# The input projection's high and low halves in one 512-column product

## The chip, the cores and the metric

The kernel runs on one core of a Trainium2 chip. The metric is the device time of one execution in microseconds. The engines are TensorE (PE in the profile, its weight loads PEld), VectorE (DVE), ScalarE (ACT), GpSimd (POOL) and SyncE (SP), whose queue here issues the transfers.

## The reference

Two layers over 256 tokens of width 2048, batch 1, all in float32:

```python
for l in range(DEPTH):
    h = rms_norm(x, norm_g[l])
    proj = jnp.einsum('btd,dc->btc', h, w_in[l])
    rw_in, g_rw, q, k_at, v_at, g_at = jnp.split(proj, col_splits, axis=-1)
    rw_in = bidir_token_shift(rw_in, shift_mu[l])
    r, k, v, xw, xa = jnp.split(rw_in, rw_splits, axis=-1)
    y_rw = rwkv7_branch(r, k, v, xw, xa, ...)        # two scans, forward and backward, 16 heads
    y_at = window_attention(rope(q), rope(k_at), v_at, sink[l])   # 16 heads, 4 KV heads
    mix = jnp.concatenate([y_rw * jax.nn.silu(g_rw), y_at * jax.nn.silu(g_at)], axis=-1)
    x = x + jnp.einsum('btc,cd->btd', mix, w_out[l])
return rms_norm(x, final_g)
```

The change touches the input projection `proj` (the second line of the loop) and the steps that take its tiles out of PSUM.

## The kernel before

**Precision.** Each float32 operand of a large product is split into a high part (rounded to TensorE's fast float32 type, fp32r) and a low part (the rest). A product is then the sum of three: high weight by high x, high weight by low x, low weight by high x. Every weight tile arrives as float32 and is split on the chip: `wsplit` has ACT write the high part `hi` (L253) and DVE the low part `lo` (L255), in pieces of 128x512.

**The stream.** A tile of the input projection is 128 output columns by 256 tokens, summed over 16 blocks of 128 rows of `w_in`. `gemm` queues a tile as 16 steps, one for each block `kk`, in two halves of 8 with one weight load (512 KB) each. A step of the old form is three products of 256 columns into a `[128, 256]` PSUM tile `pm` (L331, L332, L333). With `wide=True` a step is two products: the high weight by the high and the low part of x in one product of 512 columns (L324), then the low weight by the high part into the first 256 columns (L325); the two halves of the 512-column tile have to be added at the end. The form with `wide` needs both parts of a row side by side. `Pairs` keeps them so, four rows of `(2, 256)` in each of its tiles; `Rows` keeps eight rows of one part in a tile. Before the change only the output projection is `wide`, in its first 15 tiles of 16, with the mixed values `L.M` in `Pairs`; x is in two `Rows`, `L.XH` and `L.XL`, written by `x_split` (ACT L217, DVE L218).

**The tiles of a layer.** Two low-rank tiles (0 and 1); for each of eight pairs of recurrent heads four tiles (k, v, r and gate); the value product of attention (`v_step`, with x as the stationary operand, L600 to L602); two rotary key tiles; eight rotary query tiles and eight gate tiles. When a tile's 16 steps are done, its evacuation runs:

- `shift_evac` (k, v, r and the low-rank tiles): DVE multiplies `pm` by the norm's factor into `u` (L473), ACT scales it into the destination (L474), DVE adds the two shifted neighbours (L475, L476).
- `silu_evac` (gates): DVE multiplies by the norm's factor into `g` (L484), ACT takes a tanh (L485), DVE combines (L486).
- `rope_evac` (rotary): ACT copies `pm` into `u` (L572); four transfers on SP's queue swap its 32-partition blocks into `rrot` (L574); 13 steps later DVE turns it, 15 steps later it is split.

`ps_main` has two buffers for `pm`; the value product takes both at once.

**The order.** TensorE's program is in the order in which the kernel is written. `window(64, ...)` interleaves 64 steps of the stream (four tiles) with stages of the recurrence (`scan_p`, `scan_i`, `scan_b`) and of attention in 11 slots; after 13 such windows a layer's input tiles 2 and on are through. Then come the 256 steps of the output projection and the next layer's tiles 0 and 1. The instructions of DVE and ACT are ordered by the framework's scheduler, from the program order with priority offsets (the low weight parts and `scan_b` are raised). Each engine's queue is served in order.

Of the kernel before, what the change touches and what calls it, by code (L numbers as in the profile page):

```python
# [9 lines left out]
F32 = mybir.dt.float32  # L10
F32R = mybir.dt.float32r
# [4 lines left out]
AF = mybir.ActivationFunctionType  # L16
ALU = mybir.AluOpType
# [116 lines left out]
def hybrid_trunk_kernel(ctx, tc, xT, wi, wv, wo, par, fing, dup, iup, sink, pos, cst, out):  # L134
# [65 lines left out]

    class Pairs:

        def __init__(self):
            self.t = []
            self.more()

        def more(self):
            for tag in (("s0a", "s1a"), ("s0b", "s1b"))[len(self.t) // 2]:
                self.t.append(hold(tag, F32R, "M" + str(len(self.t)), (4, 2, T)))

        def row(self, j, part=None):
            t = self.t[j // 4][:, j % 4]
            return t.rearrange("p a t -> p (a t)") if part is None else t[:, part]

    def x_split(XH, XL, x, k, l):
        g = G0[:, k : k + 1] if l == 0 else PR[:, l, P_NG + k : P_NG + k + 1]
        A.activation(XH[:, k, :], x, AF.Copy, scale=g)  # L217
        V.scalar_tensor_tensor(XL[:, k, :], x, g, XH[:, k, :].bitcast(F32), op0=ALU.mult, op1=ALU.subtract)  # L218

    class Norm:  # L220

# [84 lines left out]

    S = Stream()

    def gemm(src, operands, evac, raws=None, begin=None, bank=None, pairs=None, wide=False):

        box = []

        def step(kk):
            def f(w):
                if not box:
                    box.append(bank() if bank else ps_main.tile([128, 2 * T if wide else T], F32, tag="m", name="pm"))
                    if begin:
                        begin()
                pm = box[0]
                k = kk % 8  # L320
                wh, wl = w[0][:, k * 128 : (k + 1) * 128], w[1][:, k * 128 : (k + 1) * 128]
                if wide:
                    m = pairs()
                    PE.matmul(pm, wh, m.row(kk), start=(kk == 0), stop=(kk == 15), skip_group_check=True)  # L324
                    PE.matmul(pm[:, 0:T], wl, m.row(kk, 0), start=False, stop=(kk == 15), skip_group_check=True)  # L325
                    return
                if pairs:
                    xh, xl = (pairs().row(kk, i) for i in range(2))
                else:
                    xh, xl = (x[:, kk, :] for x in operands())  # L330
                PE.matmul(pm, wh, xh, start=(kk == 0), stop=False)  # L331
                PE.matmul(pm, wh, xl, start=False, stop=False)  # L332
                PE.matmul(pm, wl, xh, start=False, stop=(kk == 15))  # L333
# [127 lines left out]
    def queue_inputs(l):  # L461
# [2 lines left out]
        dpm = lambda o, j: DP[:, l, o + j : o + j + 1]  # L464

        def inproj(ct, evac, **kw):
            gemm(wi[l, ct], lambda: (L.XH, L.XL), evac, **kw)

        def shift_evac(j, place):
            def evac(pm):  # L470
                dst = place()
                u = st("u", [T], bufs=2)
                V.tensor_tensor(u, pm, L.norm.rb, op=ALU.mult)  # L473
                A.activation(dst, u, AF.Identity, scale=dpm(0, j))  # L474
                V.scalar_tensor_tensor(dst[:, 1:T], u[:, 0 : T - 1], prm(P_MU0, j), dst[:, 1:T], op0=ALU.mult, op1=ALU.add)  # L475
                V.scalar_tensor_tensor(dst[:, 0 : T - 1], u[:, 1:T], prm(P_MU1, j), dst[:, 0 : T - 1], op0=ALU.mult, op1=ALU.add)  # L476

            return evac

        def silu_evac(place):  # L480
            def evac(pm):
                g = st("g", [T], bufs=2)
                th = st("g", [T], bufs=2)
                V.tensor_tensor(g, pm, L.norm.rb, op=ALU.mult)  # L484
# [67 lines left out]
            return evac  # L552

        for p, t in enumerate(L.ts):
            inproj(2 + 4 * p, shift_evac(p, new(t, "k", "kr", 4)), begin=ups(p, t))
            inproj(3 + 4 * p, value_evac(p, t))
            inproj(4 + 4 * p, shift_evac(16 + p, new(t, "r", "kr", 4)))
            inproj(5 + 4 * p, silu_evac(new(t, "gr", "vg", 8)))


        rope = []
# [1 line left out]
        def rope_evac(place):  # L563
            def evac(pm):
# [7 lines left out]
                A.activation(raw, pm, AF.Copy)  # L572
                for q in range(4):
                    SY.dma_start(out=rot[q * 32 : q * 32 + 32, :], in_=raw[(q ^ 1) * 32 : (q ^ 1) * 32 + 32, :])  # L574
                hi, lo = place()
# [17 lines left out]
        def v_step(kk, b):  # L593
            def f(w):
                if not pvs:
                    pvs.extend(ps_main.tile([128, T], F32, tag="m", name="pva") for _ in range(2))
                k = kk % 4
                wh, wl = (x[:, k * 256 : (k + 1) * 256] for x in w)
                tb = slice(b * 128, (b + 1) * 128)
                PE.matmul(pvs[b], L.XH[:, kk, tb], wh, start=(kk == 0), stop=False)  # L600
                PE.matmul(pvs[b], L.XH[:, kk, tb], wl, start=False, stop=False)
                PE.matmul(pvs[b], L.XL[:, kk, tb], wh, start=False, stop=(kk == 15))  # L602

            return f

# [19 lines left out]
            return place  # L625

        for m in range(2):
            inproj(2 + 4 * NP + m, rope_evac(k_place(m)))
        L.tq = [dict() for _ in range(8)]

        def q_place(j):
# [8 lines left out]
        for n in ("q0", "q1", "q2", "q3", "g0", "q4", "g1", "q5", "g2", "q6", "g3", "q7", "g4", "g5", "g6", "g7"):  # L640
            j = int(n[1])
            if n[0] == "q":
                inproj(QG0 + 2 * j, rope_evac(q_place(j)))
            else:
                inproj(QG0 + 2 * j + 1, silu_evac(new(L.tq[j], "g", "vg", 8)))

    def queue_output(l):

# [3 lines left out]
        def tile_of(k):  # L652
# [6 lines left out]
            def evac(pm):  # L659
# [7 lines left out]
                if k == 0:  # L667
                    to.norm = Norm()
                    to.acc = st("acc", [T])
                    if not last:  # L670
                        to.XH, to.XL = Rows("s2", F32R, "XH"), Rows("s3", F32R, "XL")
                if not last:
                    x_split(to.XH, to.XL, x, k, l + 1)
# [17 lines left out]

        for k in range(NKT):
            ev, be = tile_of(k)
            gemm(wo[l, k], None, ev, begin=be, pairs=lambda: L.M, wide=k < NKT - 1)

    def layer(l):
        L = layers[l]
        prm = lambda o, j: PR[:, l, o + j : o + j + 1]
        dpm = lambda o, j: DP[:, l, o + j : o + j + 1]
        L.M = Pairs()  # L700
        FR = hold("s0b", F32, "FR", (8 * T,))

        def mix_split(j, y, g2):
# [601 lines left out]
```

## Time and profile before

| | |
|---|---|
| median of 3 runs | 1169.26 us (1168.23 to 1169.78) |
| profiled execution | 1168.46 us, its span 1166.7 us |
| granted TensorE clock | 0.994 |
| TensorE busy, weight loads busy | 1145.5 us (98%), 1051.1 us (90%) |
| DVE busy, ACT busy | 915.9 us (79%), 785.6 us (67%) |
| steps in the old form, reading XH | 1664 |
| steps in the wide form | 480 |

The span is from the first to the last instruction; busy time is the time in which at least one instruction of the engine runs, with the tail in which it overlaps its successor. The duration of a matmul holds its way through the array, which the next one overlaps: what one costs TensorE in a stream is the distance between the starts of two. The windows of layer 0 run from about 23.8 to 496.7 us, those of layer 1 from about 599 to 1066 us; each window takes between 24 and 43 us.

### The profile page before, as it was taken

Reading aid. Unit: us, or ns where it says so; the run is one execution under the profiler, and the core shown is the slowest. Engines: PE = TensorE matmul, PEld = TensorE weight load, DVE = VectorE, ACT = ScalarE, POOL = GpSimd, SP = SyncE. Lnnn points to the kernel's source line nnn. Section 1 sums busy time; section 2 is a strip of 40 time slices with the busy share of each in tenths; the row PEclk is TensorE's granted clock in tenths of the full one; section 3 lists DMA queues with packets and bytes.
Section 4 is the critical chain, followed back from the end, with each engine's and each line's share of the span. In section 5 each row is a group of like instructions: output and inputs, shape, how many; then the busy total and the mean of one; then the engine's idle time right before and its main releaser. Section 6 shows DMA issues by size and latency. Waiting matters only on the chain.

```text
span 1166.7 us, 37155 instructions
## 1 busy us (share of the span) xinstructions
PE 1145.5 (98%) x15671; PEld 1051.1 (90%) x15671; DVE 915.9 (79%) x2042; ACT 785.6 (67%) x1986; POOL 21.7 (2%) x23
## 2 busy tenths in 40 slices
PE   8999999999999999999999999999999999999996
PEld 7998999999899998988899889999999999988885
DVE  7889978888877677767768888888887767786665
ACT  6667876787775666655556677876786666675553
POOL 0000000000000000000000000000000000000000
PEclk9999999999999999999999999999999999999998
DMA  7544434333334443477655443334333344345663
GB/s 261 169 152 134 131 103 130 97 112 111 101 116 123 126 127 122 133 235 242 217 182 171 143 136 116 100 114 126 104 112 112 120 130 130 101 150 184 211 202 126
DMA packets 60551, 166.59 MB, mean 143 GB/s; under 512 B 7744, under 2 KB 22880, under 8 KB 60384
## 3 DMA queue, kind: packets, MB, share of 16 engines
q1 hardware_dynamic: 60384, 164.21, 45.1%
q8 instruction: 123, 2.02, 0.7%
q14 instruction: 44, 0.36, 0.1%
HBM read 157.37 MB, written 4.19 MB: 138 GB/s over the span
## 4 chain that ended last, share of the span: by engine, by line
PE 76%; issue 13%; DVE 5%; ACT 4%; DMA 2%; SPq 0%; POOL 0%; POOLq 0%; DVEq 0%; ACTq 0%
PE pm L331 17%; PE pm L333 14%; PE pm L332 14%; PE pm L324 4%; PE pg L855 3%; PE pm L325 2%; PE pcc L1018 2%; DVE lo L255 2%; PE pcc L1046 2%; PE pd L962 1%; PE py L1030 1%; PE py L1003 1%; PE pq L953 1%; PE pcc L1036 1%; ACT hi L253 1%
## 5 line engine op out<-in xcount | busy, mean ns | idle before, releaser
L255 DVE TENSOR_TENSOR lo<-raw,hi 128x512 fp32r<-128x512 f32 x560 | 371.9, 686 | 103.7 <-ACT hi L253 101.6
L253 ACT ACTIVATE hi<-raw 128x512 fp32r<-128x512 f32 x560 | 329.5, 625 | 167.8 <-PE pm L324 58.4
L331 PE MATMUL pm<-XHa,hi 128*128 128x256 f32 x832 | 245.5, 295 | 0.9 <-ACT VA L609 0.4
L331 PE MATMUL pm<-XHb,hi 128*128 128x256 f32 x832 | 243.6, 293 | 0.2 <-ACT hi L253 0.2
L333 PE MATMUL pm<-XHb,lo 128*128 128x256 f32 x832 | 234.0, 281 | 1.4 <-DVE lo L255 1.4
L333 PE MATMUL pm<-XHa,lo 128*128 128x256 f32 x832 | 234.2, 281 | 1.1 <-DVE lo L255 0.8
L332 PE MATMUL pm<-XLa,hi 128*128 128x256 f32 x832 | 234.2, 282 | 0.5 <-DVE XLa L218 0.3
L332 PE MATMUL pm<-XLb,hi 128*128 128x256 f32 x832 | 234.0, 281 | 0.1
L331 PEld LDWEIGHTS pm<-XHa,hi 128*128 128x128 f32 x832 | 157.0, 189 | 11.6 <-ACT XHa L217 1.7
L324 PE MATMUL pm<-M,hi 128*128 128x512 f32 x480 | 166.9, 392 | 0.4 <-ACT hi L253 0.4
L331 PEld LDWEIGHTS pm<-XHb,hi 128*128 128x128 f32 x832 | 157.2, 189 | 5.9 <-ACT hi L253 0.4
L333 PEld LDWEIGHTS pm<-XHa,lo 128*128 128x128 f32 x832 | 157.2, 189 | 2.4 <-DVE lo L255 2.3
L333 PEld LDWEIGHTS pm<-XHb,lo 128*128 128x128 f32 x832 | 157.2, 189 | 2.1 <-DVE lo L255 2.0
L332 PEld LDWEIGHTS pm<-XLa,hi 128*128 128x128 f32 x832 | 157.3, 189 | 1.1 <-DVE XLa L218 1.1
L332 PEld LDWEIGHTS pm<-XLb,hi 128*128 128x128 f32 x832 | 157.3, 189 | 0.3 <-DVE XLb L218 0.3
L325 PE MATMUL pm<-M,lo 128*128 128x256 f32 x480 | 134.3, 280 | 0.2 <-DVE lo L255 0.2
L324 PEld LDWEIGHTS pm<-M,hi 128*128 128x128 f32 x480 | 90.1, 188 | 21.2 <-issue 0.8
L325 PEld LDWEIGHTS pm<-M,lo 128*128 128x128 f32 x480 | 90.1, 188 | 0.5 <-DVE lo L255 0.5
L1041 ACT ACTIVATE suv<-pcc 64x128 f32<-64x128 f32 x128 | 34.5, 270 | 72.3 <-PE pcc L1039 48.5
L1124 ACT ACTIVATE mv<-mv,mx 128x257 f32<-128x257 f32 x56 | 28.0, 502 | 15.1 <-DVE mx L1121 15.0
L956 ACT ACTIVATE QF<-pq 128x256 f16<-128x256 f32 x80 | 30.4, 380 | 10.5 <-PE pq L920 6.2
L855 PE MATMUL pg<-mv,FR 64*128 64x128 f32 x512 | 37.2, 285 | 0.0
(292 smaller groups left out, 2044.3 us busy)
## 6 DMA issues: line engine op xcount, KB each, us to landing
raw<-wi SPq DMA_DIRECT2D x207, 512.0 KB
raw<-wo SPq DMA_DIRECT2D x64, 512.0 KB
raw<-wv SPq DMA_DIRECT2D x8, 512.0 KB
rrot<-u SPq DMA_DIRECT2D x80, 32.0 KB
vg<-xT SPq DMA_DIRECT2D x16, 128.0 KB
xd<-vg SPq DMA_DIRECT2D x16, 128.0 KB
vg<-xd SPq DMA_DIRECT2D x16, 128.0 KB
g<-dup SPq DMA_DIRECT2D x16, 97.0 KB
```

The lines of the kernel that those rows point to most:

```text
L253: A.activation(hi[:, q], raw[:, q], AF.Copy)
L255: V.tensor_tensor(lo[:, q], raw[:, q], hi[:, q].bitcast(F32), op=ALU.subtract)
L324: PE.matmul(pm, wh, m.row(kk), start=(kk == 0), stop=(kk == 15), skip_group_check=True)
L325: PE.matmul(pm[:, 0:T], wl, m.row(kk, 0), start=False, stop=(kk == 15), skip_group_check=True)
L331: PE.matmul(pm, wh, xh, start=(kk == 0), stop=False)
L332: PE.matmul(pm, wh, xl, start=False, stop=False)
L333: PE.matmul(pm, wl, xh, start=False, stop=(kk == 15))
L855: PE.matmul(pg[:, h, c * 128 : (c + 1) * 128], BK[half[h], d, c, 1 - h : 3 - h, :].rearrange("p s j -> p (s j)"), MV[half[h], d, c].rearra ...
L956: A.activation(t_sub(QF), flat4(pq[:, :, 0:128]), AF.Copy)
L1018: PE.matmul(pc[half[h], 0, d, :], GE[h][r, d, ci[d], 0, :], SUV[r, d, ci[d], h, :], start=True, stop=True)
L1041: A.activation(here(h), pc[half[h], 1], AF.Copy)
L1124: A.activation(Sc[:, h, q, 0:257], Sc[:, h, q, 0:257], AF.Exp, scale=0.125, bias=mx[:, q : q + 1], accum_out=den[:, q : q + 1])
```

## The change

Both parts of x's rows are kept in `Pairs` (`L.X`, in the same memory as before), and `gemm` takes all its rows from a `Pairs`. All tiles but 0 and 1 of each layer run with `wide=True`: the four tiles of each pair and attention's key, query and gate tiles, 50 of 52. At the end of a wide tile ACT copies the second half of `pm` to SBUF and DVE adds the first half to it; in the pairs' and gate tiles that comes ahead of the multiply by the norm's factor, which then reads SBUF (`scaled`), and in the rotary tiles ACT's copy takes the second half and the add follows it. The value product takes its stationary operand from the same rows.

```diff
-        def __init__(self):
-            self.t = []
+        def __init__(self, name, tags):
+            self.name, self.tags, self.t = name, tags, []
             self.more()
 
         def more(self):
-            for tag in (("s0a", "s1a"), ("s0b", "s1b"))[len(self.t) // 2]:
-                self.t.append(hold(tag, F32R, "M" + str(len(self.t)), (4, 2, T)))
+            for s in self.tags:
+                i = len(self.t)
+                self.t.append(hold(s + "ab"[i // 2], F32R, self.name + str(i), (4, 2, T)))
...
-    def x_split(XH, XL, x, k, l):
+    def x_rows():
+        x = Pairs("X", ("s2", "s3"))
+        x.more()
+        return x
+
+    def x_split(X, x, k, l):
         g = G0[:, k : k + 1] if l == 0 else PR[:, l, P_NG + k : P_NG + k + 1]
-        A.activation(XH[:, k, :], x, AF.Copy, scale=g)
-        V.scalar_tensor_tensor(XL[:, k, :], x, g, XH[:, k, :].bitcast(F32), op0=ALU.mult, op1=ALU.subtract)
+        A.activation(X.row(k, 0), x, AF.Copy, scale=g)
+        V.scalar_tensor_tensor(X.row(k, 1), x, g, X.row(k, 0).bitcast(F32), op0=ALU.mult, op1=ALU.subtract)
...
                 if wide:
-                    m = pairs()
+                    m = rows()
                     PE.matmul(pm, wh, m.row(kk), start=(kk == 0), stop=(kk == 15), skip_group_check=True)
                     PE.matmul(pm[:, 0:T], wl, m.row(kk, 0), start=False, stop=(kk == 15), skip_group_check=True)
                     return
...
-            gemm(wi[l, ct], lambda: (L.XH, L.XL), evac, **kw)
+            gemm(wi[l, ct], lambda: L.X, evac, **kw)
+
+        def scaled(o, pm):
+            x = pm
+            if pm.shape[-1] > T:
+                A.activation(o, pm[:, T : 2 * T], AF.Copy)
+                V.tensor_tensor(o, o, pm[:, 0:T], op=ALU.add)
+                x = o
+            V.tensor_tensor(o, x, L.norm.rb, op=ALU.mult)
...
-                V.tensor_tensor(u, pm, L.norm.rb, op=ALU.mult)
+                scaled(u, pm)
...
-                V.tensor_tensor(g, pm, L.norm.rb, op=ALU.mult)
+                scaled(g, pm)
...
-            inproj(2 + 4 * p, shift_evac(p, new(t, "k", "kr", 4)), begin=ups(p, t))
-            inproj(3 + 4 * p, value_evac(p, t))
+            inproj(2 + 4 * p, shift_evac(p, new(t, "k", "kr", 4)), begin=ups(p, t), wide=True)
+            inproj(3 + 4 * p, value_evac(p, t), wide=True)
...
-                A.activation(raw, pm, AF.Copy)
+                A.activation(raw, pm[:, T : 2 * T], AF.Copy)
+                V.tensor_tensor(raw, raw, pm[:, 0:T], op=ALU.add)
...
-                PE.matmul(pvs[b], L.XH[:, kk, tb], wh, start=(kk == 0), stop=False)
+                PE.matmul(pvs[b], L.X.row(kk, 0)[:, tb], wh, start=(kk == 0), stop=False)
...
-            inproj(2 + 4 * NP + m, rope_evac(k_place(m)))
+            inproj(2 + 4 * NP + m, rope_evac(k_place(m)), wide=True)
...
-                inproj(QG0 + 2 * j, rope_evac(q_place(j)))
+                inproj(QG0 + 2 * j, rope_evac(q_place(j)), wide=True)
             else:
-                inproj(QG0 + 2 * j + 1, silu_evac(new(L.tq[j], "g", "vg", 8)))
+                inproj(QG0 + 2 * j + 1, silu_evac(new(L.tq[j], "g", "vg", 8)), wide=True)
```

The pairs' other two tiles (r and gate) get `wide=True` in the same way, and the callers of `x_split` pass the one object.

More of the change, by code (lines that the diff above doesn't have):

```diff
@@ L307, in hybrid_trunk_kernel, with gemm @@
     S = Stream()
-    def gemm(src, operands, evac, raws=None, begin=None, bank=None, pairs=None, wide=False):
+    def gemm(src, rows, evac, raws=None, begin=None, bank=None, wide=False):
         box = []
@@ L326, in f @@
                     return
[L327 to L330, printed above, removed]
+                xh, xl = (rows().row(kk, i) for i in range(2))
                 PE.matmul(pm, wh, xh, start=(kk == 0), stop=False)
@@ L554, in queue_inputs @@
         for p, t in enumerate(L.ts):
-            inproj(2 + 4 * p, shift_evac(p, new(t, "k", "kr", 4)), begin=ups(p, t))
-            inproj(3 + 4 * p, value_evac(p, t))
-            inproj(4 + 4 * p, shift_evac(16 + p, new(t, "r", "kr", 4)))
-            inproj(5 + 4 * p, silu_evac(new(t, "gr", "vg", 8)))
+            inproj(2 + 4 * p, shift_evac(p, new(t, "k", "kr", 4)), begin=ups(p, t), wide=True)
+            inproj(3 + 4 * p, value_evac(p, t), wide=True)
+            inproj(4 + 4 * p, shift_evac(16 + p, new(t, "r", "kr", 4)), wide=True)
+            inproj(5 + 4 * p, silu_evac(new(t, "gr", "vg", 8)), wide=True)
         rope = []
@@ L599, in f @@
                 tb = slice(b * 128, (b + 1) * 128)
-                PE.matmul(pvs[b], L.XH[:, kk, tb], wh, start=(kk == 0), stop=False)
-                PE.matmul(pvs[b], L.XH[:, kk, tb], wl, start=False, stop=False)
-                PE.matmul(pvs[b], L.XL[:, kk, tb], wh, start=False, stop=(kk == 15))
+                PE.matmul(pvs[b], L.X.row(kk, 0)[:, tb], wh, start=(kk == 0), stop=False)
+                PE.matmul(pvs[b], L.X.row(kk, 0)[:, tb], wl, start=False, stop=False)
+                PE.matmul(pvs[b], L.X.row(kk, 1)[:, tb], wh, start=False, stop=(kk == 15))
             return f
@@ L670, in evac @@
                     if not last:
-                        to.XH, to.XL = Rows("s2", F32R, "XH"), Rows("s3", F32R, "XL")
+                        to.X = x_rows()
                 if not last:
-                    x_split(to.XH, to.XL, x, k, l + 1)
+                    x_split(to.X, x, k, l + 1)
                     SY.dma_start(out=L.xd[:, k, :], in_=x)
@@ L693, in queue_output @@
             ev, be = tile_of(k)
-            gemm(wo[l, k], None, ev, begin=be, pairs=lambda: L.M, wide=k < NKT - 1)
+            gemm(wo[l, k], lambda: L.M, ev, begin=be, wide=k < NKT - 1)
     def layer(l):
@@ L699, in layer @@
         dpm = lambda o, j: DP[:, l, o + j : o + j + 1]
-        L.M = Pairs()
+        L.M = Pairs("M", ("s0", "s1"))
         FR = hold("s0b", F32, "FR", (8 * T,))
@@ L1187, in hybrid_trunk_kernel @@
     L0.norm = Norm()
-    L0.XH, L0.XL = Rows("s2", F32R, "XH"), Rows("s3", F32R, "XL")
+    L0.X = x_rows()
     for k in range(NKT):
-        x_split(L0.XH, L0.XL, X0[:, k, :], k, 0)
+        x_split(L0.X, X0[:, k, :], k, 0)
         S.run(1)
```

## The prediction

> **What bounds the kernel now.** I read the page's engine shares first, then the chain that ended last, then the waits, then the stream and the windows of the layer.
>
> ```profile
> span 1166.7 us, 37155 instructions
> ...
> PE 1145.5 (98%) x15671; PEld 1051.1 (90%) x15671; DVE 915.9 (79%) x2042; ACT 785.6 (67%) x1986; POOL 21.7 (2%) x23
> ...
> PE 76%; issue 13%; DVE 5%; ACT 4%; DMA 2%; SPq 0%; POOL 0%; POOLq 0%; DVEq 0%; ACTq 0%
> ```
>
> TensorE is busy for 98% and carries 76% of the chain; the 13% of "issue" is also mostly TensorE between two of its own instructions. DVE and ACT together carry 9%. So the time is the time that TensorE needs for its own instructions, plus few waits. The question is what one step of the weight stream costs it in the two forms, and whether the work that the change hands to ACT and DVE makes it wait.
>
> The waits whose name bears on the change:
>
> ```profile
> DVE lo L255 <- ACT hi L253: 101.6, 139, 3.1
> ...
> DVE g L484 <- PE pm L333: 25.7, 19, 2.4
> ...
> DVE u L473 <- PE pm L333: 10.9, 14, 1.5
> ...
> SPq L574 <- ACT u L572: 14.0, 4, 5.4
> ...
> PEld pm L333 <- DVE lo L255: 4.4, 9, 1.4
> ```
>
> The columns are total us, times and the longest. The last row is TensorE waiting for the low weight parts, 4.4 us in all: the weight split is just ahead of the stream nine times and otherwise well ahead. The two rows of L484 and L473 say that DVE stands at the head of its queue 33 times until TensorE ends a tile.
>
> **The step of the stream, old and new form.** The output projection already runs the 512-column form in its first 15 tiles and the three-product form in the last one, on the same kind of operands. These are TensorE's rows of the timeline, first and last of runs of steps without other work between them:
>
> ```profile
> 552.01 0.39 PE L324 MATMUL pm<-M,hi 128*128 128x512 f32 x1
> 552.24 0.28 PE L325 MATMUL pm<-M,lo 128*128 128x256 f32 x1
> ...
> 557.56 0.39 PE L324 MATMUL pm<-M,hi 128*128 128x512 f32 x1
> ...
> 581.13 0.28 PE L331 MATMUL pm<-M,hi 128*128 128x256 f32 x1
> ...
> 586.76 0.28 PE L331 MATMUL pm<-XHa,hi 128*128 128x256 f32 x1
> ```
>
> From 552.01 to 557.56 there are 16 steps of the new form: 5.55/16 = 0.347 us. From 581.13 to 586.76 there are 16 of the old form: 5.63/16 = 0.352 us. The columns streamed are the same 768, so all that goes is 5 ns a step. The third weight load goes too, but it was hidden: the rows start 0.12 us apart, not at the 0.19 us that a load is shown with.
>
> Inside the layer's windows the old form is a little slower (four steps between these rows):
>
> ```profile
> 164.45 0.28 PE L331 MATMUL pm<-XHb,hi 128*128 128x256 f32 x1
> ...
> 165.87 0.28 PE L331 MATMUL pm<-XHb,hi 128*128 128x256 f32 x1
> ```
>
> 1.42/4 = 0.355 us. If the new form runs at 0.347 there too, a step gains 8 ns; if whatever slows the windows slows both forms, it gains 5. I take 6, nearer to the pair that differs in nothing but the form.
>
> How many steps:
>
> ```profile
> L331 PE MATMUL pm<-XHa,hi 128*128 128x256 f32 x832 | 245.5, 295 | 0.9 <-ACT VA L609 0.4
> L331 PE MATMUL pm<-XHb,hi 128*128 128x256 f32 x832 | 243.6, 293 | 0.2 <-ACT hi L253 0.2
> ```
>
> 1664 steps read XH. Tiles 0 and 1 of each layer keep the old form (2 x 16 x 2 = 64), so 1600 change: 1600 x 6 ns = **9.6 us less** on TensorE, between 8.0 and 12.8.
>
> One rule of the Trainium skill says less. "TensorE: Matmul & The Clock Gate", section "Wait — 56ns, not 53.3ns?", gives the cost of a matmul beyond its columns as a fixed 2.5 ns or so, so one matmul fewer in each of 1600 steps would be an estimated 4.0 us. The trace disagrees: the sixteen-step runs above differ by 5 ns a step.
>
> **What is added.** Each of the 100 wide tiles has its two halves added: 80 (pairs' four tiles and attention's gate) get an ACT copy and a DVE add ahead of the old multiply; the 20 rotary tiles already had the ACT copy and get the add alone. The nearest rows:
>
> ```profile
> L473 DVE TENSOR_TENSOR u<-pm,rb 128x256 f32<-128x256 f32 x52 | 21.8, 421 | 11.4 <-PE pm L333 10.9
> ...
> L484 DVE TENSOR_TENSOR g<-pm,rb 128x256 f32<-128x256 f32 x32 | 13.5, 423 | 26.0 <-PE pm L333 25.7
> ...
> L572 ACT ACTIVATE u<-pm 128x256 f32<-128x256 f32 x20 | 7.4, 372 | 0.0
> ```
>
> The add has the shape of L473, one operand in PSUM: 100 x 0.42 = 42 us on DVE, to about 958 us. The copy is L572's: 80 x 0.37 = 30 us on ACT, to about 815. Neither sum reaches the span, so what counts is where DVE is already tight. The windows of the layer (one 64-step window each; PE, PEld, DVE, ACT busy):
>
> ```profile
> 50.40:78.70 28.30, 27.15 (x242) 26.08 (x240) 26.60 (x51) 20.28 (x46) 0.00 (x0) 1.00 0.51 163
> 78.70:112.30 33.60, 32.90 (x465) 30.32 (x463) 30.71 (x62) 24.57 (x57) 0.00 (x0) 1.00 0.43 132
> 149.40:189.40 40.00, 40.00 (x753) 37.08 (x751) 35.24 (x76) 30.41 (x82) 1.38 (x1) 1.00 0.36 112
> 352.60:389.30 36.70, 36.70 (x705) 33.98 (x703) 25.49 (x56) 22.61 (x63) 1.01 (x1) 1.00 0.43 127
> 463.50:496.70 33.20, 33.20 (x281) 29.96 (x281) 26.00 (x83) 22.04 (x58) 0.00 (x0) 1.00 0.46 146
> 623.70:652.40 28.70, 27.14 (x242) 26.07 (x241) 26.44 (x50) 20.27 (x46) 0.00 (x0) 1.00 0.53 162
> 652.40:685.80 33.40, 32.90 (x465) 30.34 (x463) 29.63 (x58) 24.57 (x57) 0.00 (x0) 1.00 0.42 132
> 722.90:762.80 39.90, 39.90 (x752) 37.05 (x751) 33.97 (x72) 30.40 (x82) 1.31 (x1) 1.00 0.36 113
> ```
>
> The rows from 149.40 and 722.90 are the same window of the two layers. Layer 0 has 35.24 - 33.97 = 1.27 us more DVE work in it (the rotary tables), about as much as the change adds to a window, and is 0.1 us longer. So at 88% of DVE, extra work is covered nearly whole by TensorE's 40 us. The rows from 50.40 and 623.70 are not so: DVE is at 92 to 94%, and TensorE has its one real wait of the layer there (first row layer 0, second layer 1):
>
> ```profile
> PE pbn L728 <- DVE ip L268: 1.0, 1, 1.0
> ...
> PE pbn L728 <- DVE ip L268: 1.1, 1, 1.1
> ```
>
> What an add takes from a full DVE queue is its distance to the next instruction:
>
> ```profile
> 71.09 0.42 DVE L268 TENSOR_TENSOR ip<-th,ip 128x256 fp32r<-128x256 f32 x1
> 71.42 0.42 DVE L473 TENSOR_TENSOR u<-pm,rb 128x256 f32<-128x256 f32 x1
> ```
>
> 0.33 us here, the 0.42 overlapping its successor. Four adds in a window are 1.3 us. In the window after the first (50.40, 623.70) I put 0.8 us of it on the path, because only the evacuations before the wait lengthen it (two or so of the four); in the next (78.70, 652.40; DVE 91 and 89%) 0.6 us. Twice each: 2.8 us, between 0 and 4 x 1.3 = 5.2. For the other 22 windows I take the 0.1 us that the layers' comparison shows: 2.2 us, between 0 and one add each, 22 x 0.33 = 7.3. Cost together **5.0 us**, between 0 and 12.5.
>
> **Edits that cost nothing, and their cover.** The new layout of X (high and low part of a row side by side) moves no instruction: the same ACT copy and DVE subtract a row, and attention's value product reads the same 128 columns. The accumulator takes 512 columns in a buffer that the output's tiles already size so; it is held for one copy and one add longer, some 0.8 us, against a whole tile (16 steps, 5.6 us) until it is needed. Only the value product takes both buffers at once, and the scan's products stand between. In the rotary tiles the partition swap (four transfers on SP's queue) now waits for the add as well, 0.4 us and its place in DVE's queue; SP already stands there for the copy (14.0 us in four waits), and behind it are weight loads. In those windows DVE is at 69 to 78% (rows from 352.60 and 463.50) and TensorE, busy in the whole of both, nowhere waits for low parts, so this is covered; uncovered it would be 0.4 x 20 = 8 us. In the pairs' tiles ACT now waits for the end of the tile where DVE did (36.6 us in 33 waits), and the high weight parts queue behind it. That is the cover that could fail; see the third rival.
>
> **The sum.** 9.6 - 5.0 = 4.6 us less. The profiled execution took 1168.46 us around its span of 1166.7, and would take 1163.9; the median of the runs, 1169.26, is 0.8 above it and becomes **1164.7**. By the fixed cost of the Trainium skill's page alone the sum would be 5.0 - 4.0 = 1.0 us more, 1170.3.
>
> **The rivals.**
> 1. All of the added work is covered and the gain is whole: 1169.3 - 9.6 = 1159.7, between 1156.5 and 1161.3. For it: the layers' comparison, and the 1.7 us in which DVE is still idle in the tightest window. Against it: TensorE waits for DVE just there.
> 2. The step gains only half as much among the layer's other work: 2.5 ns, 4.0 us, which the 5.0 us of cost consume: 1170.3, no change that a measurement shows (0.2%, 2.3 us, is about what can be told from none). For it: the slower steps in the windows, whose cause no row names. Against it: that slowing is in the old form and nothing says that the new one has more of it. The fixed cost per matmul of the Trainium skill's page (above) comes to the same.
> 3. Slower: the copy at the head of ACT's queue waits for the tile's end, the high parts behind it come later, then the low ones, and TensorE waits for those (L333's row, nine times now). It decides from 9.6/100 = 0.096 us for each wide tile. If each of the pairs' 64 tiles costs one add's 0.33 us, it is 21.1 - 9.6 = 11.5 more: 1180.8. For it: DVE's 36.6 us at that place, ACT at 76% in the full windows. Against it: 4.4 us of such waits now, and the tenth of a microsecond between the layers.
>
> **The numbers.** Forecast 0.46 (2.4 to 8 us less), first rival 0.22, second 0.16, third 0.16. Faster by over 0.2% is forecast and first rival less a little of the forecast's upper edge, 0.66; within 0.2%, 0.18; slower, 0.16. The range runs from the full gain without cost, 12.8 less (1156.5, rounded to 1157), to the smallest gain with the largest cost, 12.5 - 8.0 = 4.5 more (1173.8, rounded to 1174); what it leaves out is most of the third rival. The forecast's own range is 1161 to 1167.
>
> **What would show it.** Right: steps of 0.347 to 0.349 us in the windows; 1600 matmuls and as many weight loads fewer; DVE near 958, ACT near 815 us; the windows from 149 on some 0.3 us shorter each, those from 50 and 624 no shorter, with a longer wait of pbn for DVE. Wrong: "pm <- DVE lo" well above 4.4 us, or "ACT u <- PE pm" followed by late high parts (third rival); steps of 0.35 (second).

## The result: slower, and the profile after

The changed kernel takes 1199.19 us (median of 6 runs, 1196.68 to 1207.24) beside 1168.35 us (6 runs, 1168.11 to 1169.78) of the kernel before on the same chip: a ratio of 1.0273, 95% interval 1.025 to 1.0295, about 32 us more where 4.6 less were forecast. In the runs below, a ratio is always to the kernel before on the same chip, with its 95% interval behind it; 0.1% is 1.17 us.

The changed kernel's page (span, busy time, chain that ended last):

```profile
span 1197.0 us, 34084 instructions
...
PE 1147.2 (96%) x14071; PEld 966.5 (81%) x14071; DVE 948.4 (79%) x2142; ACT 811.7 (68%) x2066; POOL 22.3 (2%) x23
...
PE 64%; issue 14%; ACT 9%; DVE 8%; DMA 3%; SPq 1%; POOL 0%; DVEq 0%; POOLq 0%; ACTq 0%
```

TensorE has its 1600 matmuls fewer, and DVE and ACT have the work that was forecast (958 and 815 us said, 948 and 812 measured), with room left by their shares. What changed is the chain: TensorE carries 64% of it where it carried 76%, DVE and ACT 17% where they carried 9%. That is time in which TensorE waits. The waits (total us, times, longest):

```profile
PE py L1078 <- DVE ysq L274: 12.2, 8, 2.2
...
PE pm L330 <- ACT hi L259: 6.9, 2, 3.8
...
PE pm L331 <- DVE lo L261: 4.9, 8, 1.2
...
DVE u L274 <- DMA rrot<-u: 17.1, 10, 3.4
```

The first row is new: before, no wait of a `py` product (the transposes of a pair's normalised result) for `ysq` was in the list. In the windows (columns as in the prediction's; the windows of a layer are counted from 0, and window n streams pair n's four tiles up to 7): window 9 of layer 0, then 1, 2 and 4 of layer 1.

```profile
369.30:407.50 38.20, 36.44 (x641) 30.11 (x639) 26.21 (x59) 21.64 (x61) 1.05 (x1) 1.00 0.37 116
640.40:673.90 33.50, 29.35 (x178) 24.50 (x177) 27.53 (x53) 21.52 (x50) 0.00 (x0) 0.90 0.46 147
673.90:708.40 34.50, 32.62 (x401) 26.48 (x399) 31.18 (x63) 25.73 (x60) 0.00 (x0) 1.00 0.42 129
746.70:787.90 41.20, 39.75 (x689) 33.39 (x687) 35.33 (x76) 31.90 (x86) 1.37 (x1) 1.00 0.35 109
```

Beside the prediction's rows of the same windows: 38.2 for 36.7, 33.5 for 28.7, 34.5 for 33.4, 41.2 for 39.9. In the last, TensorE was busy for the whole 39.90 and now is idle for 1.45. In the second the granted clock is 0.90. Summed over both layers (distances between the first steps of the windows, after less before):

| stretch | us more |
|---|---|
| start, up to window 0 | 1.1 |
| window 1, both layers | 10.7 |
| window 2, both layers | 2.1 |
| windows 3 to 7, both layers (ten) | 15.6 |
| window 9, both layers | 3.0 |
| all others | -2.2 |
| span | 30.3 |

So there are three main places, and all have a longer evacuation in them.

**Windows 3 to 7: the v tile's evacuation stands ahead of `ysq`.** DVE's timeline of the kernel before, in layer 1's window 5 (start, us, what):

```profile
781.94 0.17 DVE L1058 TENSOR_SCALAR yv<-yv 128x4 f32<-128x4 f32 x1
...
783.89 0.48 DVE L475 SCALAR_TENSOR_TENSOR vg<-u,PR,vg 128x255 f32<-128x255 f32 x1
...
784.88 0.48 DVE L476 SCALAR_TENSOR_TENSOR vg<-u,PR,vg 128x255 f32<-128x255 f32 x1
785.28 0.41 DVE L268 TENSOR_TENSOR ysq<-py,yv 128x256 f32<-128x256 f32 x1
```

TensorE's product that reads `ysq` comes close behind:

```profile
785.95 0.66 PE L1066 MATMUL py<-C,ysq 64*64 64x64 f32 x16
```

`ysq` ends at 785.69, so 0.26 us were all the slack that it had. DVE of the changed kernel, in the same window:

```profile
807.40 0.16 DVE L1070 TENSOR_SCALAR yv<-yv 128x4 f32<-128x4 f32 x1
...
808.47 0.41 DVE L476 TENSOR_TENSOR u<-u,pm 128x256 f32<-128x256 f32 x1
...
809.40 0.42 DVE L478 TENSOR_TENSOR u<-u,rb 128x256 f32<-128x256 f32 x1
...
811.00 0.48 DVE L486 SCALAR_TENSOR_TENSOR vg<-u,PR,vg 128x255 f32<-128x255 f32 x1 [0.58 <-ACT vg L485]
811.52 0.48 DVE L487 SCALAR_TENSOR_TENSOR vg<-u,PR,vg 128x255 f32<-128x255 f32 x1
811.92 0.42 DVE L274 TENSOR_TENSOR ysq<-py,yv 128x256 f32<-128x256 f32 x1
```

From `yv` to `ysq` it was 3.34 us and is 4.52. The tile's evacuation now goes ACT (copy), DVE (add, L476), DVE (multiply, L478), ACT (scale), DVE (neighbour adds, L486 and L487), and `ysq` stands behind the neighbour adds in DVE's queue. At 810.4 to 811.0 DVE stands still at the head of its queue for ACT's scale, though `ysq` does not need it. TensorE, from the changed kernel's timeline:

```profile
810.64 0.30 PE L974 MATMUL pd<-QF,tt 64*64 64x32 f16 x16
812.40 0.68 PE L1078 MATMUL py<-C,ysq 64*64 64x64 f32 x16 [1.45 <-DVE ysq L274]
```

In layer 0's windows 4, 5 and 6 the wait for `ysq` is 2.19, 1.66 and 2.19 us. Behind the first two TensorE runs at half its clock for 3.41 us (from 184.21 and 228.58 us), behind the third it does not; the windows are 3.4, 2.0 and 1.9 us longer. The last section comes back to this.

**Window 1: late parts, then half the clock.** The changed kernel's TensorE in layer 1:

```profile
655.89 0.39 PE L330 MATMUL pm<-X,hi 128*128 128x512 f32 x1
...
656.24 0.39 PE L330 MATMUL pm<-X,hi 128*128 128x512 f32 x1
...
659.80 0.79 PE L330 MATMUL pm<-X,hi 128*128 128x512 f32 x1 [3.06 <-ACT hi L259]
...
662.31 0.63 PE L330 MATMUL pm<-X,hi 128*128 128x512 f32 x1
...
662.95 0.63 PE L330 MATMUL pm<-X,hi 128*128 128x512 f32 x1
```

The steps are 0.35 us apart, as forecast, up to the stall of 3.06 us for high weight parts that ACT writes late; after it they are 0.64 apart. ACT's rows of `hi` around the stall:

```profile
653.00 0.63 ACT L259 ACTIVATE hi<-raw 128x512 fp32r<-128x512 f32 x1 [2.31 <-DMA raw<-wi]
...
659.14 1.65 ACT L259 ACTIVATE hi<-raw 128x512 fp32r<-128x512 f32 x3
```

Between them ACT is hardly idle; the tile's added copy, the scale of the v tile and the recurrence's operations stand there in its queue. At the same place in the kernel before it was 4.8 us, behind two pieces and not one. Whether the order in the queue or the late weight transfer (2.31 us) is to blame was not taken apart.

Two stretches of 4 us show why the steps behind the stall are slow (the figure 1.00, 0.83 and so on is the granted clock):

```profile
656.00:660.00 4.00, 0.94 (x6) 0.58 (x4) 2.26 (x6) 3.93 (x13) 0.00 (x0) 0.83 0.00 0
660.00:664.00 4.00, 3.73 (x11) 2.86 (x12) 4.00 (x10) 1.55 (x4) 0.00 (x0) 0.50 0.47 131
```

The stall costs twice: the wait, and then a TensorE at half its clock. Over the whole run the mean granted clock fell from 0.994 to 0.983; worked out from these, 0.006 x 1166.7 = 7 us and 0.017 x 1197.0 = 20 us of full clock were missing, so at most 13 of the 30 us are this second cost (some of it lies in the stalls themselves). The Trainium skill, "TensorE: Matmul & The Clock Gate", section "What's actually happening", says that the clock drops to half after an idle window of about 3.4 us and comes back after as long a busy one. The trace agrees on the half clock; on what sets it off, see the last section.

**Window 9: DVE waits for the partition swap of the rotary tile.** Changed kernel, DVE:

```profile
955.61 0.43 DVE L274 TENSOR_TENSOR u<-u,TW 128x256 f32<-128x256 f32 x1 [3.28 <-DMA rrot<-u]
...
956.75 1.22 DVE L873 TENSOR_TENSOR ge<-pg,C 128x1024 f32<-128x1024 f32 x1
```

and TensorE:

```profile
958.02 0.59 PE L891 MATMUL pt<-C,FR 64*128 64x64 f32 x12 [0.90 <-DVE ge L873]
```

The swap starts an add later, DVE stands 3.28 us for it, and the multiply that TensorE's transposes need (`ge`) is behind. A second wait of 0.9 us, for `tt`, follows in the window.

### The profile page after: what moved, and what is told of

The parts are those of the page before. It is cut to its first block, busy times and chain, and to the rows that moved or that the text cites. A ratio compares the mean times of both kernels' runs of the same rounds, so it can differ in the third digit from the quotient of the medians.

```text
span 1197.0 us, 34084 instructions
## 1 busy us (share of the span) xinstructions
PE 1147.2 (96%) x14071; PEld 966.5 (81%) x14071; DVE 948.4 (79%) x2142; ACT 811.7 (68%) x2066; POOL 22.3 (2%) x23
## 4 chain that ended last, share of the span: by engine, by line
PE 64%; issue 14%; ACT 9%; DVE 8%; DMA 3%; SPq 1%; POOL 0%; DVEq 0%; POOLq 0%; ACTq 0%
PE pm L330 27%; PE pm L331 13%; PE pg L867 3%; ACT hi L259 2%; DVE lo L261 2%; PE pcc L1030 2%; PE pcc L1058 1%; PE py L1042 1%; PE py L1015 1%; PE pd L974 1%; PE pcc L1048 1%; DMA raw<-wi 1%; PE pq L965 1%; DMA rrot<-u 1%; PE pva L612 1%
## 5 line engine op out<-in xcount | busy, mean ns | idle before, releaser
L330 PE MATMUL pm<-X,hi 128*128 128x512 f32 x1600 | 595.3, 409 | 7.3 <-ACT hi L259 6.9
L331 PE MATMUL pm<-X,lo 128*128 128x256 f32 x1600 | 452.2, 283 | 5.1 <-DVE lo L261 4.9
L330 PEld LDWEIGHTS pm<-X,hi 128*128 128x128 f32 x1600 | 303.7, 190 | 80.5 <-ACT hi L259 7.5
L331 PEld LDWEIGHTS pm<-X,lo 128*128 128x128 f32 x1600 | 304.8, 191 | 8.7 <-DVE lo L261 8.4
L976 DVE CAST_PREDICATED tv<-LV,pd 128x256 f16<-128x256 uint8 x80 | 34.3, 429 | 6.3 <-PE pd L974 5.2
L1071 POOL TENSOR_TENSOR yv<-yv,mhalf 128x4 f32<-128x4 f32 x16 | 19.9, 1241 | 848.2 <-DVE yv L1070 848.2
L867 PEld LDWEIGHTS pg<-mv,FR 64*128 64x128 f32 x512 | 31.1, 187 | 2.3 <-issue 1.0
L965 PEld LDWEIGHTS <-AB 64*64 64x64 f16 x1280 | 20.8, 107 | 14.6 <-issue 9.0
L965 PE MATMUL pq<-tv,AB 64*64 64x32 f16 x1280 | 28.3, 185 | 2.6 <-DVE tv L958 2.0
L1060 DVE TENSOR_TENSOR suv<-pcc,pc 64x128 f32<-64x128 f32 x96 | 27.5, 286 | 4.1 <-PE pcc L1058 2.5
```

The lines of the kernel that those rows point to most:

```text
L867: PE.matmul(pg[:, h, c * 128 : (c + 1) * 128], BK[half[h], d, c, 1 - h : 3 - h, :].rearrange("p s j -> p (s j)"), MV[half[h], d, c].rearra ...
L965: PE.matmul(narrow(pq[:, d], h ^ d, c), hq(AB, d, c, h), sub(TC, h, d, c, d * b), start=True, stop=True)
L976: V.copy_predicated(t_sub(TC), t_mask, flat4(pd[:, :, 0:128]))
L1060: V.tensor_tensor(here(h, i + 1), pS[half[h]], pick(PC, half[h], i, [2 * NC - 1 - 2 * i, 2], [0, 64]), op=ALU.mult)
```

## The experiments

Window lengths of layer 1 in all runs, in us, from the first step of a window to the first of the next:

| kernel | 1 | 2 | 5 | 9 | ratio |
|---|---|---|---|---|---|
| before | 28.76 | 33.37 | 39.86 | 36.67 | 1 |
| after | 33.52 | 34.45 | 41.17 | 38.18 | 1.0273 |
| e1 first half only | 31.35 | 32.95 | 39.54 | 36.29 | 0.9939 |
| e2 three products | 30.40 | 34.78 | 43.07 | 36.67 | 1.0216 |
| e3 v tiles old | 32.06 | 34.11 | 39.73 | 37.82 | 1.0075 |
| e4 attention only | 28.36 | 33.35 | 39.86 | 38.43 | 1.0026 |
| e8 v tiles only | 30.42 | 33.86 | 41.40 | 36.67 | 1.0168 |
| e9 v adds behind | 33.12 | 34.43 | 39.82 | 38.03 | 1.0088 |
| e12 no v, no rotary | 32.48 | 34.10 | 39.71 | 36.67 | 1.0047 |
| e14 pair 1 old too | 31.72 | 33.45 | 39.73 | 36.67 | 1.0021 |
| e16 gate of pair 0 old too | 28.54 | 33.43 | 39.71 | 36.67 | 0.9969 |
| e7 pairs from 3 | 28.61 | 33.39 | 39.73 | 36.67 | 0.9968 |
| e13 e7 and v behind | 28.78 | 33.40 | 39.83 | 36.67 | 0.9987 |
| e15 e7 and rotary | 28.54 | 33.41 | 39.73 | 36.55 | 0.9984 |

My theory after the comparison: the product gains what was forecast, and the evacuations lose it, by their place in the queues and not by their amount. The first rival: it is the product (its 512 columns, its double PSUM tile). The second: the added work of 72 us on DVE and ACT as such.

### The product alone, and the evacuation alone

**e1_first_half_only** has the wide products with an evacuation as short as before: the second half of `pm` is never read, so high weight by low x is left out.

```diff
-                A.activation(o, pm[:, T : 2 * T], AF.Copy)
-                V.tensor_tensor(o, o, pm[:, 0:T], op=ALU.add)
-                x = o
+                x = pm[:, 0:T]
...
-                A.activation(raw, pm[:, T : 2 * T], AF.Copy)
-                V.tensor_tensor(raw, raw, pm[:, 0:T], op=ALU.add)
+                A.activation(raw, pm[:, 0:T], AF.Copy)
```

> The changed kernel with its 512-column products, but the evacuation reads only the first half of the accumulator (no copy, no add: it leaves out high weight by low x, so the values are those of two products). Theory A (the copy and the add lengthen each evacuation, and what stands behind them in the queues of DVE, ACT and SP reaches TensorE late): all of the loss goes and the saving of the products is left, 1168.4 - 9.6 = 1159, between 1156 and 1161. Theory B (the long product or x's new layout is itself worse beside the recurrence): most of the 31 us stay, 1185 or more.

Measured: 1160.13 us, 0.9939 (0.9915 to 0.9962), 7.1 us less, between 4.4 and 9.9. Its window 4 of layer 1, in which TensorE never waits, is 0.4 shorter by the row:

```profile
722.80:762.30 39.50, 39.50 (x689) 33.24 (x687) 33.83 (x72) 30.43 (x82) 1.01 (x1) 1.00 0.37 113
```

By the table window 5 went from 39.86 to 39.54, 0.32 us over 64 steps or 5.0 ns a step, and window 9 from 36.67 to 36.29, 5.9 ns a step. So the product is not what costs. But even here window 1 is 2.6 us longer, with no instruction added: TensorE waits 2.3 us there for `ip` instead of 1.1, and the granted clock behind it is low:

```profile
644.00:648.00 4.00, 3.53 (x12) 3.10 (x13) 2.94 (x6) 1.66 (x4) 0.00 (x0) 0.62 0.47 164
```

In that window DVE sets the end (26.4 us busy of 28.7 before, and of 31.4 here); a faster TensorE only arrives earlier, waits longer and then runs at half its clock.

**e2_three_products** is the opposite: the evacuation of the change, and the 512-column product cut into two of 256 into the two halves.

```diff
+                    if split:
+                        PE.matmul(pm[:, 0:T], wh, m.row(kk, 0), start=(kk == 0), stop=(kk == 15), skip_group_check=True)
+                        PE.matmul(pm[:, T : 2 * T], wh, m.row(kk, 1), start=False, stop=(kk == 15), skip_group_check=True)
+                    else:
...
-            gemm(wi[l, ct], lambda: L.X, evac, **kw)
+            gemm(wi[l, ct], lambda: L.X, evac, split=True, **kw)
```

> The changed kernel with the long product cut into two of 256 columns, one into each half of the accumulator; copy and add as in the changed kernel, result the same. Theory A: the loss stays and the saving of the products goes, 1199 + 9 = 1208, between 1199 and 1212. Theory B: back near before, 1168 to 1175.

Measured: 1193.73 us, 1.0216 (1.0201 to 1.0232). Four fifths of the loss (0.0216 of 0.0273) are there with the old three products; the wait for `ysq` is 11.9 us in 8 waits (12.2 in 8 in the changed kernel). Theory B falls, and theory A misses its range of 1199 to 1212 too: the changed kernel is the slower one, by 6.7 us (0.0057), although its steps are shorter: its windows 1 and 9 are 3.1 and 1.5 us longer than e2's (layer 1). The shorter steps are used up there by the waits and the clock. (Window 5 of e2 is long because 3.41 us of half clock, from 808.59 us, follow its wait for `ysq`.)

### The v tiles

**e3_v_tile_old** takes the 16 v tiles out of the change, **e8_v_only** leaves only them in, and **e9_v_adds_behind** keeps the whole change, with the v tile's two neighbour adds 8 steps later, behind `ysq`.

The edits of e3 and of e9:

```diff
-            inproj(3 + 4 * p, value_evac(p, t), wide=True)
+            inproj(3 + 4 * p, value_evac(p, t))
```

```diff
-            ev = shift_evac(8 + p, new(t, "v", "vg", 8))
+            ev = shift_evac(8 + p, new(t, "v", "vg", 8), late=8)
...
+                if late:
+                    S.later(late, adds)
+                else:
+                    adds()
```

In e8 the k, r, gate and rotary tiles and attention's gates lose their `wide=True`.

> The changed kernel with the pairs' v tiles (16 of 100) in the old form. Theory A, in the detail that the v tile's neighbour add stands in DVE's queue ahead of the recurrence's ysq and that TensorE waits for ysq in the full windows (12.2 us in eight waits): these waits go, 16 tiles lose 1.5 us of saving, 1199 - 12 + 1.5 = 1188 or less. If the loss is spread evenly over the tiles instead: 1199 - 0.16 x 31 = 1194.

> Only the 16 v tiles wide, all others in the old form: 32 of the 100 added instructions of DVE and ACT at most. If the v tile's own chain decides: the full windows cost their 1.5 us again although DVE has only one added instruction there, 1168.4 + 8 x 1.5 - 1.5 = 1179, between 1175 and 1186. If it takes the load of all tiles: 1167 to 1171.

> The changed kernel, all tiles wide, with the two neighbour adds of the v tiles issued eight steps later, so that they stand behind the recurrence's ysq in DVE's queue instead of ahead of it; nothing else is changed, and no work is taken away. If TensorE's 12 us of waiting for ysq come from these two adds standing at the head of DVE's queue until ACT has written the v tile: the waits go, the full windows of layer 1 fall from 41.2 to about 39.7 us each, and the time from 1199 to about 1183 (between 1178 and 1187). If ysq is late because DVE has too much work: 1195 or more.

Measured: e3 1177.3 us, 1.0075 (1.0058 to 1.0092); e8 1188.21, 1.0168 (1.0143 to 1.0193); e9 1179.97, 1.0088 (1.0073 to 1.0103). So 16 tiles of 100 cost 19.6 us by themselves (0.0168 x 1168.7), and without them the change is 23 us cheaper (0.0198). e3 and e9 are as the theory said; e8 lies 2 us above the range that I gave. e8's wait:

```profile
PE py L1077 <- DVE ysq L274: 11.8, 8, 2.1
```

e9 has the same instructions as the changed kernel, in another order: the adds are moved, and with them the scheduler has placed some others differently, on DVE and on ACT. Its timeline on DVE in window 5 of layer 1:

```profile
792.56 0.16 DVE L1077 TENSOR_SCALAR yv<-yv 128x4 f32<-128x4 f32 x1
...
794.55 0.42 DVE L478 TENSOR_TENSOR u<-u,rb 128x256 f32<-128x256 f32 x1
794.89 0.41 DVE L274 TENSOR_TENSOR ysq<-py,yv 128x256 f32<-128x256 f32 x1
...
796.82 0.47 DVE L488 SCALAR_TENSOR_TENSOR vg<-u,PR,vg 128x255 f32<-128x255 f32 x1
```

`ysq` follows `yv` after 2.33 us (4.52 in the changed kernel, 3.34 before), TensorE's wait for it is gone from the list, and the window is back at 39.82 us. The reordering is worth 21.6 us (1.0273 less 1.0088) with all the work left in: the price of these tiles is, nearly all of it, a place in a queue and not their work. That it is the place of the two adds, and not of the others that moved with them, rests on the wait: the 12.2 us for `ysq` went, and with them the half clock behind two of these waits. Of the work some 0.3 us a full window are left (39.82 beside 39.54 in e1, which has none of the added instructions). The Trainium skill, "TensorE: Matmul & The Clock Gate", section "Architectural detail: the array is 16× 32×32, not 1× 128×128", says that ACT and DVE serve their queues strictly in order; the wait of 0.58 us at 811.00 agrees, with `ysq` ready behind it (POOL had written its last factor by about 809.1).

### Attention alone

**e4_attention_only** has only attention's 36 tiles wide; the four lines of the pairs lose their `wide=True`.

> Only attention's 36 tiles wide, the pairs' in the old form. Theory A: the windows of the recurrence are as before, attention's tiles save 36 x 16 x 6 ns = 3.5 us and the rotary turn behind its later transfers costs 1.5 us in one window of each layer: 1168, within 1165 to 1170. If the loss is spread evenly over the tiles: 1168.4 + 0.36 x 31 = 1179.5.

Measured: 1171.48 us, 1.0026 (1.0015 to 1.0036), 3.0 us slower and above the range that I gave (1165 to 1170). Window 9 is 38.09 and 38.43 us in the two layers (36.67 before); windows 8, 10 and 12 are 0.2 to 0.5 shorter each. The steps' gain is there and window 9 gives more back.

### The rest: k, r and gates

**e12_no_v_no_rotary** leaves v and rotary tiles old (64 tiles wide). **e7_pairs_from_3** is e12 with k, r and gates wide in pairs 3 to 7 alone (46 tiles); its edit for k, with r and the gate likewise:

```diff
-            inproj(2 + 4 * p, shift_evac(p, new(t, "k", "kr", 4)), begin=ups(p, t), wide=True)
+            inproj(2 + 4 * p, shift_evac(p, new(t, "k", "kr", 4)), begin=ups(p, t), wide=p > 2)
```

> The pairs' k, r and gate tiles and attention's gate tiles wide (64 of the 100), v and rotary tiles in the old form. From the run without wide v tiles (1177.3), less the rotary turn's 1.5 us in two windows: 1174.5, between 1172 and 1177. What is left above 1168.4 - 6.1 sits in the second and third window of each layer.

> As the one before, but of the pairs' k, r and gate tiles only those of pairs 3 to 7 wide (46 tiles), so that the second and third window of each layer are as before. If the loss that remains sits there: 46 x 16 x 6 ns = 4.4 us less than before, 1164, between 1163 and 1167. If the added instructions cost everywhere: 1169 or more.

Measured: e12 1174.6 us, 1.0047 (1.0033 to 1.006); e7 1165.36, 0.9968 (0.9955 to 0.9981), 0.3% faster. Window 9 is at 36.67 in both, as the rotary tiles are old; window 1 is long in e12 (31.87 and 32.48) and short in e7 (28.37 and 28.61). So what is left of the loss, some 9 us, comes from nine tiles a layer. Two more runs looked for which of them.

**e14_all_but_pair_1** (`wide=p != 1`) is e12 with pair 1's k, r and gate old too, which window 1 itself streams.

> k, r and gate tiles of all pairs but pair 1 wide, attention's gates wide; v and rotary tiles old. Theory (window 1 of a layer is lost by its own tiles' copies, that hold up the high weight parts behind them on ScalarE): window 1 is back at 28.3 to 28.8 us in both layers (e12 31.9 and 32.5), window 2 stays at 34 to 34.6, ratio 0.998 to 1.000. Rival (the loss comes from the work of windows 0 and 2 that surrounds it, or from the whole of the first three pairs): window 1 stays above 30.5, ratio 1.002 to 1.005.

Measured: 1171.09 us, 1.0021 (1.001 to 1.0033). My theory fell: window 1 is still 31.43 and 31.72 us, so it is not its own tiles alone that hold it up. The wait has changed, though: in e12 TensorE stands there for `hi`, 2.2 us in each layer, and in e14 no longer for `hi` but for `ip`. e14's row of the window, its wait, and the clock behind that:

```profile
624.40:656.10 31.70, 28.67 (x242) 27.59 (x241) 26.80 (x51) 20.98 (x47) 0.00 (x0) 0.95 0.47 153
```

```profile
PE pbn L739 <- DVE ip L274: 4.5, 2, 2.2
```

```profile
646.00:650.00 4.00, 2.57 (x12) 2.57 (x13) 3.67 (x6) 0.78 (x2) 0.00 (x0) 0.67 0.68 218
```

It is the wait for `ip` that was 1.1 us before, now 2.2. `ip` ends a chain that DVE works off from the window's first instruction on, and there stands the evacuation of the gate tile of pair 0, the last tile of window 0. DVE in e14:

```profile
625.12 0.69 DVE L261 TENSOR_TENSOR lo<-raw,hi 128x512 fp32r<-128x512 f32 x1 [2.29 <-ACT hi L259]
625.73 0.42 DVE L476 TENSOR_TENSOR g<-g,pm 128x256 f32<-128x256 f32 x1
...
626.67 0.42 DVE L478 TENSOR_TENSOR g<-g,rb 128x256 f32<-128x256 f32 x1
...
629.87 1.27 DVE L274 TENSOR_TENSOR_SCAN FR<-MSK,FR 128x256 f32<-128x256 f16 x2
```

**e16_gate_of_pair_0_old** makes that one tile a layer old again:

```diff
-            inproj(5 + 4 * p, silu_evac(new(t, "gr", "vg", 8)), wide=p != 1)
+            inproj(5 + 4 * p, silu_evac(new(t, "gr", "vg", 8)), wide=p > 1)
```

> The kernel of e14 with one tile a layer more in the old form: the gate tile of pair 0, the last tile of window 0, which is evacuated at the start of window 1. Theory (window 1 is set by VectorE's queue, which is full from its start to the product ip that TensorE waits for; the gate's copy and add stand at the head of that queue ahead of the scan, and each microsecond there is one at its end): window 1 is 28.3 to 28.9 us in both layers (e14 31.4 and 31.7), the wait of pbn for ip back at 1.0 to 1.3 us (e14 2.2), no half clock in it, ratio 0.996 to 0.998. Rival (the k and r tiles of pair 0 or the tiles of pair 2 lengthen it too, by the work they add): window 1 stays above 30 us, ratio 1.000 to 1.002.

Measured: 1165.27 us, 0.9969 (0.9957 to 0.9981), and window 1 is 28.50 and 28.54 us. Its window, wait and DVE:

```profile
622.60:651.20 28.60, 27.29 (x243) 26.22 (x241) 26.44 (x50) 20.34 (x46) 0.00 (x0) 1.00 0.55 170
```

```profile
PE pbn L739 <- DVE ip L274: 2.2, 2, 1.1
```

```profile
622.78 0.42 DVE L478 TENSOR_TENSOR g<-pm,rb 128x256 f32<-128x256 f32 x1 [1.80 <-PE pm L336]
...
626.92 1.21 DVE L274 TENSOR_TENSOR_SCAN FR<-MSK,FR 128x256 f32<-128x256 f16 x2
```

The scan starts 4.3 us after the window's begin (626.92 - 622.60) and 5.5 in e14 (629.87 - 624.40): 1.2 us, which is by what the wait for `ip` grows. Two tiles with 0.08 us of gain each (16 steps of 5.0 ns) cost 6 us (1.0021 less 0.9969): 1.1 us of wait a window, and 1.7 by the 3.41 us of half clock that follow the longer wait. This is shown with pair 1's tiles old. No run has them wide and pair 0's gate tile old, so what they cost by themselves, and with it the changed kernel's own wait for `hi` in window 1, stays open.

### Back on top of the best

**e13_pairs3_v_behind** is e7 with the v tiles of pairs 3 to 7 wide and their adds behind `ysq`; **e15_pairs3_rotary** is e7 with the rotary tiles wide.

> The kernel of e7 (k, r and gate tiles of pairs 3 to 7 and attention's gates wide) with the v tiles of those five pairs wide too, their two neighbour adds 8 steps later on VectorE, behind the square that TensorE waits for. Theory (the price of a wide v tile is the place of its adds in VectorE's queue, not its work): windows 3 to 7 stay at 39.7 to 39.8 us, no wait of py for ysq of more than 1 us in all, ratio 0.995 to 0.998, beside 0.9968 of e7. Rival (the added copy and add of the v tile cost by their work on full engines): 1 to 1.5 us more in each of ten windows, ratio 1.005 to 1.01.

> The kernel of e7 with the 20 rotary tiles wide too. Theory (the rotary add puts the partition swap later, and VectorE stands at the head of its queue for it in window 9): window 9 is 37.8 to 38.4 us (e7 36.7), VectorE's wait for the swap is 15 to 18 us in all (e7 8.0), and the 1.9 us of shorter steps are used up: ratio 0.997 to 1.000. Rival (the swap's delay is covered, as predicted): window 9 at 36.5, 1.9 us less than e7, ratio 0.994 to 0.996.

Measured: e13 1167.81 us, 0.9987 (0.9978 to 0.9997); e15 1166.81, 0.9984 (0.9975 to 0.9993). Both miss in part. In e13 layer 1's windows are where the theory had them (39.81 to 39.83, no wait for `ysq`), but they are 0.1 longer than e7's 39.72, where 16 shorter steps should have made them as much shorter; in layer 0 windows 4 to 6 are 0.35 longer. A v tile with its adds behind thus gains nothing, and its ratio is higher than the 0.995 to 0.998 that I gave. Of the difference of the profiled spans (1167.1 and 1163.6) these ten windows hold 1.8 us; 0.6 lie ahead of the first window and 1.0 in the first half of layer 0's output projection, and what causes those is open.

In e15 window 9 is long in layer 0 and as forecast in the prediction in layer 1:

```profile
350.40:389.10 38.70, 36.39 (x641) 30.06 (x639) 26.38 (x60) 21.88 (x62) 1.29 (x1) 1.00 0.38 112
...
919.20:955.70 36.50, 36.32 (x640) 30.06 (x638) 26.27 (x58) 22.11 (x62) 1.01 (x1) 1.00 0.39 120
```

DVE's longest wait for the swap is 3.6 us in the first and 2.1 in the second, and TensorE waits behind the first 1.2 us for `ge` and 1.1 for `tt`, behind the second 0.2 for `tt`. So the swap's delay is covered or not by a margin of one or two microseconds, and the same window can fall on either side; what decides it between the layers is open. In e2, with the longer steps, window 9 was covered in both.

## Why the prediction was wrong

**Right: the step.** I took 6 ns for each of 1600 steps (9.6 us, between 8.0 and 12.8). e1 shows 5.0 ns in window 5 and 5.9 in window 9, so 8.0 to 9.4 us: its profiled span is 3.0 us shorter than before's (1163.7, 1166.7), after 5.1 us lost again in its two windows 1 (30.92 and 31.35 for 28.38 and 28.76). The second rival's 2.5 ns would have made window 5 shorter by 0.16 us and not by 0.32. With it falls, for these products, the fixed cost of the Trainium skill's page, "TensorE: Matmul & The Clock Gate", section "Wait — 56ns, not 53.3ns?".

**Nearly right: the amounts.** DVE has 32.5 us more where I said 42, ACT 26.1 where I said 30. An add takes the 0.33 us to its successor, as the prediction itself measured, and not the 0.42 that the sum of 42 used.

**Wrong: the term "Cost together 5.0 us, between 0 and 12.5".** It measured about 39 us (1.0273 less e1's 0.9939). I had sized it by the load: how much DVE work a window holds, and that 1.27 us more of it in layer 0's windows cost 0.1. As far as the waits of before show, that extra work stood ahead of nothing that TensorE waits for. The added instructions do: they lie in the chain ACT, DVE, ACT, DVE of one evacuation, and behind its last link in DVE's queue stands `ysq`. The windows from 149 on, where I took 0.1 us (at most 0.33) and steps that save 0.3, are 1.2 to 1.3 us longer in layer 1 and up to 3.4 in layer 0, where half the clock follows two of the waits. The prediction named what frees the PSUM buffer ("held for one copy and one add longer, some 0.8 us, against a whole tile") and not what is queued behind each evacuation; the rows for it, `yv` and `ysq` around the v tile's adds, were in the trace of before.

**Wrong by its size: window 1.** I priced 0.8 us a window, and it was 6.0 in layer 0 (28.38 to 34.33) and 4.8 in layer 1. "a longer wait of pbn for DVE" was named and is the mechanism of e14 (1.1 to 2.2 us), where the evacuation that counts is not among "two or so of the four" of the window but the last of the window before. In the changed kernel itself TensorE stands there for `hi` (3.8 and 3.06 us) and for `ip` less than before (0.3 and 0.7 us); that is the third rival's wait, and why ACT is late is open. And a stall of 2 to 3 us can be followed by half the clock, which the sum had nowhere. The trace of before has it: "TensorE has its one real wait of the layer there" overlooks 1.81 us for `tt` at 293.4 us, in window 7 of layer 0, with 3.41 us of half clock from 295.92. That window takes 43.3 us and layer 1's 39.9.

**Wrong: "so this is covered" of the rotary swap.** Window 9 is 1.5 us longer in both layers of the changed kernel; e4 and e15 show that the cover is short by a microsecond or two, in three of their four windows. What I named as cover, that TensorE is nowhere short of low parts there, was not what stands behind DVE's wait: that is `ge`.

**The third rival** had the sign. Its mechanism, late high and low parts, is in the trace (6.9 us for `hi`, 4.9 for `lo`), and costs most in window 1; but e8 and e9 put 20 us of the loss on the v tiles' adds, which no rival named, and the time went beyond its 1180.8. An even price for each of "the pairs' 64 tiles" is wrong too: 16 v tiles cost 19.6 us, two gate tiles 6, and the 46 tiles of e7 gain 3.7.

## What to carry to other kernels

In this kernel an instruction added to a chain across two in-order engines was priced by what stands behind each of its links in those queues and who waits for that, not by the engine's free share: look up the next instruction that the bounding engine needs, and compare its slack with the longer chain. Apply such a change tile by tile: here 46 or 56 of 100 tiles give the gain (e7, e16: 0.9968 and 0.9969), and some of the rest lose ten times what their product saves, or more. Where another engine sets the end of a stretch, a faster TensorE gains nothing there and can lose, by a longer stall and the clock after it (e1's window 1).

## What the hardware showed that I had not expected

TensorE's clock falls to half behind stalls shorter than I thought. Behind the 3.06 us for `hi` the granted clock was 0.50 (660 to 664 us of the changed kernel); behind 2.2 and 2.3 us for `ip` it was 0.67 and 0.62 over 4 us (e14, e1); behind the 1.45 us for `ysq` in layer 1's full windows and the 1.1 us for `ip` of e16 it stayed at 1.00.

The length of the stall alone does not decide it. In each of the 14 profiled runs all changes of the granted clock lie on a grid of 3.41 us (in the changed kernel 184.21, 228.58 and 658.66 us are 13 and 126 such intervals apart). Two stalls of 2.19 us in the changed kernel, by intervals of that grid (columns as in the windows above):

```profile
180.80:184.21 3.41, 1.22 (x29) 0.84 (x29) 2.39 (x7) 3.29 (x13) 0.00 (x0) 1.00 0.41 126
184.21:187.62 3.41, 3.41 (x29) 2.89 (x26) 2.71 (x9) 1.70 (x4) 0.00 (x0) 0.50 0.09 32
...
266.13:269.54 3.41, 1.88 (x26) 1.41 (x24) 2.38 (x6) 3.28 (x12) 0.01 (x1) 1.00 0.39 125
269.54:272.95 3.41, 2.75 (x34) 2.41 (x35) 3.19 (x10) 2.62 (x7) 0.00 (x0) 1.00 0.32 125
```

The first stall lies in one interval, in which TensorE is idle for 2.19 us, and the next interval has half the clock. The second is cut by the grid into 1.53 and 0.66 us, and the clock stays. Over all 14 runs, without their first 40 and last 20 us, each of the 21 full-clock intervals with 1.7 us or more of idle TensorE is followed by half the clock, 5 of the 13 with 1.4 to 1.7 us are, and none with less. So what counts here is the idle time within one interval, and where a stall falls on the grid is luck. The page of the Trainium skill "TensorE: Matmul & The Clock Gate", section "What's actually happening", gives an idle window of about 3.4 us; here an interval of that length that was idle for half was enough.
